# Index products of the sample tokens in 64x32 tiles, eight together, with buffers of their own for key/value turns and spread scores, and a third count on ScalarE

## The chip, the cores and the metric

One NeuronCore of a Trainium2 chip runs the whole kernel. The metric is the device time of one execution in microseconds. The kernel before took 988.06 us (median of three runs, 987.04 to 989.44).

The engines are named as in the profile: PE is TensorE, DVE is VectorE, ACT is ScalarE, POOL is GpSimd, SP is SyncE, which issues most DMAs. L913 is line 913 of the kernel.

## What is computed

The reference is one inference step of a hybrid decoder layer for 1024 prompt tokens and for 8 sequences of 4 sample tokens each (with 8192 past tokens in pages of 128). After an RMSNorm and one big input projection, a sparse attention and a retention run side by side; an output projection and a gate follow. The change touches how the sample tokens choose the 256 past tokens that they attend to:

```
def _index_select(qi, wi, ki, qpos, kpos, topk):
    s = jnp.einsum('bqhd,bsd->bqhs', qi, ki) * (D_IDX ** -0.5)     # 8 index heads, 64 wide
    score = jnp.einsum('bqh,bqhs->bqs', wi, jax.nn.relu(s))
    score = jnp.where(valid, score, -jnp.inf)
    top_val, top_idx = lax.top_k(score, topk)
```

For a sample sequence b, q runs over its 4 tokens and s over its 8192 past tokens, whose index keys lie in pages of a cache; so 32 rows (4 tokens x 8 heads) of 64 numbers meet 8192 keys. Besides, the prompt's own top 256 are found by a search that counts scores over a threshold, and the keys and values of the prompt are written out in token order.

## The kernel before

The kernel goes through stages in this order (times of the profiled execution): the norm, the transposes and the index projections and scores of the prompt (0 to 155 us); the **sample-index stage** (155 to 292 us); the retention (to about 555 us); the attention (to about 740 us); the output projection and the gate (to the end). The program is written as Python that emits instructions; a scheduler of the framework, which works on its own model of the time, then orders the instructions of each engine. Engines go through their instructions in that order and wait on one another by semaphores. issue_after (L880, L923) ties an instruction's place behind another's.

In the sample-index stage the loop at L904 goes through 16 page pairs (8 sequences, two halves a). For each:

- key_pages (L433) fetches 128 x 2048 numbers, 1 MB, by an indirect DMA that POOL issues (L437), into a slab kx. There are two slabs, so a load waits until the slab's last user is done.
- DVE turns the two halves of the slab by 32x32 blocks (L911, up = 0 and 1). The first result goes to the slab's free third, the second to a tile kT of its own.
- PE multiplies the queries with them (L913, into a pair of PSUM banks called pox; there are two such pairs). The stationary operand qbd is 128 x 64 per sequence: it holds the 32 query columns twice, for row half 0 in columns 0 to 31 and for row half 1 in columns 32 to 63, with zeros elsewhere. Each product takes all 128 rows and 64 columns of the array and streams 512 columns; the two for one half of the slab (u2 = 0 and 1) use the two column halves of the array. So a pair has 4 products (8 matmul records in the trace, since an fp32 matmul leaves two).
- ACT empties the banks with a Relu into rl (L916).

After two pairs, head_sum (L876) weighs and adds the heads: four products into the four 32-row strips of a bank py (L879, L882), a copy ys (L884), and a DMA to xt_d. Later by_key (L888) turns ys once more (xv, L890), spreads it on POOL (xe, L892) and writes it to xs_d. rn, ys, xv and xe share a ring of two buffers.

Between these, unit() runs the input projections of the queries (qa), keys and values (kava), and the gate (ga): a unit is 24 matmuls into a bank pb (L286 to L288) for 384, 416 or 256 tokens, and a consumer. Those of keys and values call use_kv (L462): a copy of pb into kvs on ACT (L465), and before the next unit turn_kv (L469): PE transposes (L474, into kvt), a copy back into the second half of kvs on DVE (L476), and one DMA of it to the output (L478; L497 writes values once more to v_d). kvs, qst (queries), kst (keys) and sga (gate) all take their buffers from one ring of two, tag qst.

The prompt's search (bisect_prompt) is stepped in between as well. A round counts, for six blocks of 128 prompt tokens, how many scores pass a threshold. The two longest blocks (1024 and 896 scores) are counted on ACT (L737, js), the other four on DVE (L739, jk); excess (L742) joins the counts on DVE, and a new threshold W follows. NA is the number of blocks counted on ACT.

Of the kernel before, what the change touches and what calls it, by code (L numbers as in the profile page):

```python
# [11 lines left out]
F32 = mybir.dt.float32  # L12
# [5 lines left out]
ALU = mybir.AluOpType  # L18
# [29 lines left out]
def _const_table():  # L48
# [15 lines left out]
    put("caus", caus)  # L64
    put("wsel", ((p // 8 % 4 * 4 + p // 32)[:, None] == np.arange(32)[None, :]) * 1.0)
    put("slots", np.tile(np.arange(256.0), (128, 1)))
# [65 lines left out]
def tile_step(ctx: ExitStack, tc: tile.TileContext, I, O):  # L132
# [271 lines left out]
    sx0 = sxs.enter_context(pool("sx0"))  # L404
    qbd = sx0.tile([128, 8, 64], F32, name="qbd")
    nc.gpsimd.memset(qbd, 0.0)
    kis = sx0.tile([64, NS], F32, name="kis")
    qsn = sx0.tile([64, 8, NS], F32, name="qsn")

    def q_sample_index(j, pt):  # L410
        for o in range(2):
            s = pt[o * 64:o * 64 + 64, 384:416].rearrange("p (b t) -> p b t", b=8)
            for r in range(2):
                d = qbd[r * 64:r * 64 + 64].rearrange("p b (r t h) -> p r b t h", r=2, h=8)
                nc.vector.tensor_scalar(d[:, r, :, :, 2 * j + o], s, 0.125, None, op0=ALU.mult)
            nc.vector.tensor_scalar(qsn[:, 2 * j + o, :], pt[o * 64:o * 64 + 64, 384:416], 0.125, None, op0=ALU.mult)
# [45 lines left out]
    def use_kv(g, pt, outs, outp, new, then=lambda tk: None):  # L462

        st = qsp.tile([128, 2, 416], F32, tag="qst", bufs=2, name="kvs")
        nc.scalar.copy(st[:, 0, :GRP[g][1]], pt[:, :GRP[g][1]])  # L465
        turn.append(lambda: then(turn_kv(g, st, outs, outp, new)))

    def turn_kv(g, st, outs, outp, new):
# [6 lines left out]
        nb = NP[g]  # L475
        nc.vector.tensor_copy(st[:, 1, :nb], tp[:, :nb])  # L476
        tk = st[:, 1, :nb].rearrange("p (b c) -> p b c", c=128)
# [218 lines left out]
    NB = 6  # L696
    NA = 2

# [157 lines left out]
    def step(gen, n=1):  # L856
        for _ in range(n):
# [4 lines left out]

    wst = sx.tile([128, 8, 32], F32, name="wst")
    nc.vector.tensor_tensor(wst, wcol[:, :, None].to_broadcast([128, 8, 32]),
                            C("wsel")[:, None, :].to_broadcast([128, 8, 32]), op=ALU.mult)
    pn = bank("pn", "t")
# [9 lines left out]
    def head_sum(b, rls):  # L876
        py = bank("py")

        last_ = nc.tensor.matmul(py[96:128, :], wst[:, b, :], rls[3], start=True, stop=True)  # L879
        with tc.issue_after(last_.ins):  # L880
            for i in range(3):
                nc.tensor.matmul(py[32 * i:32 * i + 32, :], wst[:, b, :], rls[i], start=True, stop=True)  # L882
        ys = sx.tile([128, 512], F32, tag="ys", bufs=2, name="ys")
        nc.scalar.copy(ys, py)  # L884
        nc.sync.dma_start(xt_d[b], ys)
        pend.append(lambda: by_key(b, ys))

    def by_key(b, ys):  # L888
        xv = sx.tile([128, 512], F32, tag="ys", bufs=2, name="xv")
        nc.vector.transpose(xv, ys)  # L890
        xe = sx.tile([128, 8, 16, 2], F32, tag="ys", bufs=2, name="xe")
        nc.gpsimd.tensor_copy(xe.rearrange("p c k r -> p k c r"),  # L892
# [11 lines left out]
    for b in range(8):  # L904
        rls = []
        for a in range(2):
            kx = key_pages(2 * b + a) if b else kxs[a]
            po = pair("pox")
            for up in range(2):
                kT = kx[:, 2048:] if up == 0 else sx.tile([128, 1024], F32, tag="kT", bufs=1, name="kT")  # L910
                nc.vector.transpose(kT, kx[:, up * 1024:up * 1024 + 1024])  # L911
                for u2 in range(2):
                    nc.tensor.matmul(po[u2 * 64:u2 * 64 + 64, up * 512:up * 512 + 512], qbd[:, b, :],  # L913
                                     kT[:, u2 * 512:u2 * 512 + 512], start=True, stop=True)
            rl = sx.tile([128, 1024], F32, tag="rl", bufs=3, name="rl")
# [1164 lines left out]
```

## Time and profile before

| | |
|---|---|
| median of the runs | 988.06 us (987.04 to 989.44) |
| the profiled execution | 981.7 us, span 979.9 us |
| mean granted clock of PE | 0.991 |
| busy, share of the span | PE 95%, DVE 65%, ACT 46%, POOL 33% |
| sample-index stage, 155 to 292 us | PE 129.6, DVE 106.7, ACT 56.0, POOL 38.3 of 137 us |

The profile is that of one execution. Its rows give, per line, engine and pair of tiles, how often an instruction ran and how long it took; a bracket behind a row says how long the engine stood idle before it and which instruction ended that wait. The chain view follows the work that ended last backwards through what released it. The granted clock is the share of full speed that PE was allowed. Matmuls overlap, so the distance between the starts of two of them says more than the length of one.

### The profile page before, as it was taken

What the parts mean: (1) busy time and instruction counts of PE and PEld (TensorE: products, weight loads), DVE (VectorE), ACT (ScalarE), POOL (GpSimd) and SP (SyncE); (2) the same over time, 40 slices, a digit from 0 to 9 for tenths busy, and PEclk for the clock granted to TensorE, in tenths of its full rate; (3) what the DMA queues carried; (4) which work ended last, traced back from release to release, by engine and by line L of the source; (5) the groups of instructions that cost most, each with busy time, mean ns of one, the idle gap of its engine ahead of it and who ended that gap; (6) DMA issues with size and microseconds to landing.
All of it is one profiled execution on the core that took longest, in us unless ns stands there. A gap on an engine that the chain in (4) does not pass through costs nothing.

```text
span 979.9 us, 18935 instructions
## 1 busy us (share of the span) xinstructions
PE 927.9 (95%) x6980; PEld 788.2 (80%) x6980; DVE 640.3 (65%) x1917; ACT 450.9 (46%) x1002; POOL 319.3 (33%) x443
## 2 busy tenths in 40 slices
PE   4999999799999999999999978999999999999998
PEld 3988888567668988898989865666668999999998
DVE  6847768788945669988885577887644224953332
ACT  5646564345323886425334365565555334432210
POOL 4205112313406414415335136354414422033300
PEclk9999999899999999999999979999999999999999
DMA  8314225757534110333147226343212222512211
GB/s 267 121 67 112 71 65 181 268 171 250 161 128 107 44 44 24 88 76 79 33 132 200 83 67 183 100 124 85 61 58 80 93 66 76 176 64 88 94 35 38
DMA packets 102127, 104.36 MB, mean 107 GB/s; under 512 B 22002, under 2 KB 92210, under 8 KB 99602
## 3 DMA queue, kind: packets, MB, share of 16 engines
q1 hardware_dynamic: 96274, 76.93, 26.4%
q0 software_dynamic: 5760, 26.22, 8.8%
q8 instruction: 55, 0.90, 0.4%
q14 instruction: 38, 0.31, 0.1%
HBM read 80.36 MB, written 22.76 MB: 105 GB/s over the span
## 4 chain that ended last, share of the span: by engine, by line
PE 73%; DVE 11%; DMA 8%; ACT 4%; issue 2%; SPq 1%; POOL 0%; DVEq 0%; ACTq 0%; POOLq 0%
PE pb L286 5%; PE pb L288 4%; PE pb L287 4%; PE ob L1845 3%; PE ptp L1837 3%; PE pg L296 3%; PE pg L298 3%; PE pg L297 3%; PE pvg L296 3%; PE pvg L297 3%; PE pvg L298 3%; PE pqk L296 3%; PE pqk L297 3%; PE pqk L298 2%; PE po L296 2%; PE po L297 2%
## 5 line engine op out<-in xcount | busy, mean ns | idle before, releaser
L1308 POOL DMA_INDIRECT kvs<-in_cache_kv,idx x64 | 65.7, 1027 | 93.0 <-ACT pT L1842 29.6
L296 PE MATMUL pvg<-whi_vgb,xh 128*128 128x256 f32 x256 | 75.1, 293 | 0.6 <-DVE rp L1144 0.6
L296 PE MATMUL pqk<-whi_qkb,xh 128*128 128x256 f32 x256 | 73.4, 287 | 1.7 <-DVE rp L1144 1.2
L297 PE MATMUL pvg<-wlo_vgb,xh 128*128 128x256 f32 x256 | 73.7, 288 | 0.8 <-POOL wlo_vgb L201 0.8
L297 PE MATMUL pqk<-wlo_qkb,xh 128*128 128x256 f32 x256 | 73.6, 287 | 0.0
L296 PE MATMUL po<-whi_o,yTh 128*128 128x256 f32 x256 | 73.2, 286 | 0.2 <-ACT yTh L1892 0.2
L298 PE MATMUL pvg<-whi_vgb,xl 128*128 128x256 f32 x256 | 73.3, 286 | 0.0
L297 PE MATMUL po<-wlo_o,yTh 128*128 128x256 f32 x256 | 72.8, 284 | 0.0
L296 PE MATMUL pg<-whi_g,yTh 128*128 128x256 f32 x256 | 72.7, 284 | 0.0
L298 PE MATMUL po<-whi_o,yTl 128*128 128x256 f32 x256 | 72.7, 285 | 0.0
L298 PE MATMUL pqk<-whi_qkb,xl 128*128 128x256 f32 x256 | 72.7, 284 | 0.0
L298 PE MATMUL pg<-whi_g,yTl 128*128 128x256 f32 x256 | 72.3, 283 | 0.0
L297 PE MATMUL pg<-wlo_g,yTh 128*128 128x256 f32 x256 | 72.2, 282 | 0.0
L1824 ACT ACTIVATE L<-L,mn 128x128 f32<-128x128 f32 (+7 forms) x64 | 49.7, 777 | 19.4 <-DVE mn L1820 18.9
L201 POOL TENSOR_TENSOR wlo_g<-wraw_g,whi_g 128x256 fp32r<-128x256 f32 x32 | 27.2, 881 | 87.9 <-ACT whi_g L200 87.7
L2035 DVE TENSOR_TENSOR sgm<-pu,sgm 128x256 f32<-128x256 f32 x32 | 13.6, 424 | 64.2 <-PE pu L298 60.8
L296 PEld LDWEIGHTS pqk<-whi_qkb,xh 128*128 128x128 f32 x256 | 48.2, 188 | 3.2 <-issue 1.8
L296 PEld LDWEIGHTS po<-whi_o,yTh 128*128 128x128 f32 x256 | 49.0, 191 | 2.0 <-issue 1.6
L296 PEld LDWEIGHTS pvg<-whi_vgb,xh 128*128 128x128 f32 x256 | 48.4, 189 | 2.7 <-PE pvg L305 0.8
L296 PEld LDWEIGHTS pg<-whi_g,yTh 128*128 128x128 f32 x256 | 48.7, 190 | 1.6 <-issue 1.6
L1837 PEld LDWEIGHTS ptp<-cst,L 128*128 128x128 f32 x288 | 31.6, 142 | 22.6 <-issue 18.7
L297 PEld LDWEIGHTS pvg<-wlo_vgb,xh 128*128 128x128 f32 x256 | 48.3, 189 | 1.6 <-POOL wlo_vgb L201 1.0
(540 smaller groups left out, 3058.3 us busy)
## 6 DMA issues: line engine op xcount, KB each, us to landing
wraw_qkb<-in_w_in SPq DMA_DIRECT2D x16, 256.0 KB
wraw_vgb<-in_w_in SPq DMA_DIRECT2D x16, 256.0 KB
qas<-qas_d SPq DMA_DIRECT2D x8, 512.0 KB
wraw_o<-in_w_out SPq DMA_DIRECT2D x8, 512.0 KB
xr<-in_x_prompt SPq DMA_DIRECT2D x8, 512.0 KB
wraw_g<-in_w_ple_gate SPq DMA_DIRECT2D x8, 512.0 KB
out_y_prompt<-sgm SPq DMA_DIRECT2D x32, 128.0 KB
qas_d<-qst SPq DMA_DIRECT2D x8, 384.0 KB
```

Source lines behind the costliest of these rows:

```text
L201: nc.gpsimd.tensor_tensor(lo[:, k, :n], raw, hi[:, k, :n].bitcast(F32), op=ALU.subtract)
L286: nc.tensor.matmul(pt[:m, :n], wh, xh[:, k, ts], start=(k == 0), stop=False)
L287: nc.tensor.matmul(pt[:m, :n], wh, xl[:, k, ts], start=False, stop=False)
L288: nc.tensor.matmul(pt[:m, :n], wl, xh[:, k, ts], start=False, stop=(k == KC - 1))
L296: nc.tensor.matmul(pt[:, :n], ah, hi[:, k, :n], start=(k == 0), stop=False)
L297: nc.tensor.matmul(pt[:, :n], ah, lo[:, k, :n], start=False, stop=False)
L298: nc.tensor.matmul(pt[:, :n], al, hi[:, k, :n], start=False, stop=(k == kc - 1))
L1308: return nc.gpsimd.indirect_dma_start(out=dst, out_offset=None, in_=kvflat, in_offset=bass.IndirectOffsetOnAxis(ap=idx, axis=0))
L1824: behind[0] = nc.scalar.activation(L[:, :n], L[:, :n], AF.Exp, bias=least, scale=-1.0, accum_out=sm[:, i4:i4 + 1])
L1837: nc.tensor.transpose(tp[:, i4 * 128:i4 * 128 + 128], P[i4][:, kb * 128:kb * 128 + 128], ident)
L1845: nc.tensor.matmul(ob[64 * o:64 * o + 64, :256], vtok[:, kb, kv * 64:kv * 64 + 64], pT[:, o * 256:o * 256 + 256], start=(kb == 0), stop=(k ...
L2035: nc.vector.tensor_tensor(sg[:rows], usrc, sg[:rows], op=ALU.mult)
```

## The change

- The stationary operand becomes 64 rows by 32 columns: qbd is 128 x 8 x 32, each row half holds the 32 query columns, and there are no zeros to clear. Each page pair now has eight products (L920 in the changed kernel), one for each half of the slab (up), each 512 columns (u2) and each row half (r). Each has its own place among the array's two row halves and four column strips; up = 1 comes first, and each later product is put behind the first one.
- Both turns of a slab (L911) now come ahead of the products, and both results stay in the slab, so kT is gone and a slab is in use until all eight products are through.
- The row halves of up = 1 write swapped strips, so the rows of rl are ordered otherwise for it. wsel and wst, which pick the heads' weights, get a second version (wsel1), and head_sum uses wst[:, 1] for up = 1.
- kvs leaves the qst ring for one buffer of its own, and the copy back from kvt moves from DVE to ACT (L477 now).
- xe leaves the ys ring for one buffer of its own.
- NA goes from 2 to 3: the block with 768 scores is counted on ACT.

```
-    put("wsel", ((p // 8 % 4 * 4 + p // 32)[:, None] == np.arange(32)[None, :]) * 1.0)
+    for up in range(2):
+        slot = p // 8 % 4 * 4 + p // 32 % 2 * 2 + (p // 64 ^ up)
+        put(f"wsel{up}", (slot[:, None] == np.arange(32)[None, :]) * 1.0)
...
-    qbd = sx0.tile([128, 8, 64], F32, name="qbd")
-    nc.gpsimd.memset(qbd, 0.0)
+    qbd = sx0.tile([128, 8, 32], F32, name="qbd")
...
-        st = qsp.tile([128, 2, 416], F32, tag="qst", bufs=2, name="kvs")
+        st = sx.tile([128, 2, 416], F32, tag="kvs", bufs=1, name="kvs")
...
-        nc.vector.tensor_copy(st[:, 1, :nb], tp[:, :nb])
+        nc.scalar.copy(st[:, 1, :nb], tp[:, :nb])
...
-    NA = 2
+    NA = 3
...
-        last_ = nc.tensor.matmul(py[96:128, :], wst[:, b, :], rls[3], start=True, stop=True)
+        last_ = nc.tensor.matmul(py[96:128, :], wst[:, 1, b, :], rls[3], start=True, stop=True)
...
-                nc.tensor.matmul(py[32 * i:32 * i + 32, :], wst[:, b, :], rls[i], start=True, stop=True)
+                nc.tensor.matmul(py[32 * i:32 * i + 32, :], wst[:, i % 2, b, :], rls[i], start=True, stop=True)
...
-        xe = sx.tile([128, 8, 16, 2], F32, tag="ys", bufs=2, name="xe")
+        xe = sx.tile([128, 8, 16, 2], F32, tag="xe", bufs=1, name="xe")
...
+            kT = (kx[:, 2048:], kx[:, :1024])
             for up in range(2):
-                kT = kx[:, 2048:] if up == 0 else sx.tile([128, 1024], F32, tag="kT", bufs=1, name="kT")
-                nc.vector.transpose(kT, kx[:, up * 1024:up * 1024 + 1024])
+                nc.vector.transpose(kT[up], kx[:, up * 1024:up * 1024 + 1024])
+            head = None
+            for up in (1, 0):
                 for u2 in range(2):
-                    nc.tensor.matmul(po[u2 * 64:u2 * 64 + 64, up * 512:up * 512 + 512], qbd[:, b, :],
-                                     kT[:, u2 * 512:u2 * 512 + 512], start=True, stop=True)
+                    for r in range(2):
+                        o, rr = 32 * (2 * (r ^ up) + u2), slice(r * 64, r * 64 + 64)
+                        with (tc.issue_after(head) if head else ExitStack()):
+                            mm = nc.tensor.matmul(po[o:o + 32, up * 512:up * 512 + 512], qbd[rr, b, :],
+                                                  kT[up][rr, u2 * 512:u2 * 512 + 512], start=True, stop=True,
+                                                  tile_position=(64 * r, o))
+                        head = head or mm.ins
```

The order of the instructions moves with it. PE's order is the same up to the stage's second group of products and again in the retention; inside the stage, and in parts of the attention, it differs. Of the 16 page pairs, 13 now have their eight products in one piece; three are split by other work on PE (seven and one, five and three, three and five).

First PE, at the fourth page pair (the first unit of the keys and values ends just before, the second follows). Before, each half of a slab has its products (x2) by itself, and those of the fifth pair's first half come behind py:

```order
L288 MATMUL pb<-xh,wlo_kava 128x384
L913 MATMUL pox<-kx,qbd 64x512 x2
L913 MATMUL pox<-kT,qbd 64x512 x2
L879 MATMUL py<-rl,wst 32x512
L882 MATMUL py<-rl,wst 32x512 x3
L913 MATMUL pox<-kx,qbd 64x512 x2
L474 MATMUL kvt<-cst,kvs 128x128 x3
L286 MATMUL pb<-xh,whi_kava 128x416
```

After the change, at the same place (the eighth product of the third pair and all eight of the fourth):

```order
L290 MATMUL pb<-xh,wlo_kava 128x384
L920 MATMUL pox<-kx,qbd 32x512 x9
L881 MATMUL py<-rl,wst 32x512
L884 MATMUL py<-rl,wst 32x512 x3
L475 MATMUL kvt<-cst,kvs 128x128 x3
L288 MATMUL pb<-xh,whi_kava 128x416
```

The products of a pair have come together, and no product of the fifth pair stands ahead of kvt any more.

Then ACT at the same place, with the engines and queues that each instruction waits for. Before, the first copy into kvs:

```order
L487 CAST kst_1801<-pb_1776 128x384 [waits DMAHW4_49,PE_49]
L465 COPY kvs_1805<-pb_1776 128x384 [waits DMAHW6_49,DVE_49]
L916 ACTIVATE rl_1938<-pox_1930 128x1024 [waits PE_49]
L884 COPY ys_1824<-py_1819 128x512 [waits PE_49]
L737 ACTIVATE js_1717,cnt_1597<-score_97,W_1594 128x1024 [waits DVE_49]
L737 ACTIVATE js_1719,cnt_1597<-score_97,W_1594 128x896 [waits Activation_49]
```

After:

```order
L466 COPY kvs_1811<-pb_1782 128x384 [waits DVE_49]
L738 ACTIVATE js_1723,cnt_1600<-score_97,W_1597 128x1024 [waits DVE_49,Activation_49]
L925 ACTIVATE rl_1950<-pox_1939 128x1024 [waits PE_49]
L738 ACTIVATE js_1725,cnt_1600<-score_97,W_1597 128x896 [waits Activation_49]
L886 COPY ys_1833<-py_1828 128x512 [waits PE_49]
L477 COPY kvs_1811<-kvt_1859 128x384 [waits PE_49]
L738 ACTIVATE js_1727,cnt_1600<-score_97,W_1597 128x768 [waits Activation_49]
```

The first copy has lost its wait for a DMA queue (DMAHW), a third count has come in, and so has the copy back from kvt.

Last, ACT a little further on, in the units of keys and values that follow. Before:

```order
L487 CAST kst_1922<-pb_1897 128x256 [waits DMAHW4_49]
L465 COPY kvs_1926<-pb_1897 128x256 [waits DMAHW5_49,DVE_49,PE_49]
L465 COPY kvs_2021<-pb_1996 128x384 [waits DMAHW7_49,PE_49,Activation_49]
L737 ACTIVATE js_1956,cnt_1597<-score_97,W_1594 128x1024 [waits DVE_49]
L737 ACTIVATE js_1958,cnt_1597<-score_97,W_1594 128x896 [waits Activation_49]
L465 COPY kvs_2055<-pb_2030 128x416 [waits DMAHW0_49,PE_49]
```

After:

```order
L466 COPY kvs_1935<-pb_1906 128x256 [waits DMAHW6_49]
L477 COPY kvs_1935<-kvt_2003 128x256 [waits PE_49]
L738 ACTIVATE js_1968,cnt_1600<-score_97,W_1597 128x1024 [waits DVE_49,Activation_49]
L738 ACTIVATE js_1970,cnt_1600<-score_97,W_1597 128x896 [waits Activation_49]
L738 ACTIVATE js_1972,cnt_1600<-score_97,W_1597 128x768 [waits Activation_49]
L466 COPY kvs_2033<-pb_2008 128x384 [waits DMAHW0_49]
L477 COPY kvs_2033<-kvt_2035 128x384 [waits PE_49]
```

Each copy into kvs now waits for the DMA that writes out the unit before it, since there is one buffer, and the copy out of kvt stands between.

More of the change, by code (lines that the diff above doesn't have):

```diff
@@ L413, in q_sample_index @@
             for r in range(2):
-                d = qbd[r * 64:r * 64 + 64].rearrange("p b (r t h) -> p r b t h", r=2, h=8)
-                nc.vector.tensor_scalar(d[:, r, :, :, 2 * j + o], s, 0.125, None, op0=ALU.mult)
+                d = qbd[r * 64:r * 64 + 64].rearrange("p b (t h) -> p b t h", h=8)
+                nc.vector.tensor_scalar(d[:, :, :, 2 * j + o], s, 0.125, None, op0=ALU.mult)
             nc.vector.tensor_scalar(qsn[:, 2 * j + o, :], pt[o * 64:o * 64 + 64, 384:416], 0.125, None, op0=ALU.mult)
@@ L861, in tile_step @@
     sx = sxs.enter_context(pool("sx", side="right"))
-    wst = sx.tile([128, 8, 32], F32, name="wst")
-    nc.vector.tensor_tensor(wst, wcol[:, :, None].to_broadcast([128, 8, 32]),
-                            C("wsel")[:, None, :].to_broadcast([128, 8, 32]), op=ALU.mult)
+    wst = sx.tile([128, 2, 8, 32], F32, name="wst")
+    for up in range(2):
+        nc.vector.tensor_tensor(wst[:, up], wcol[:, :, None].to_broadcast([128, 8, 32]),
+                                C(f"wsel{up}")[:, None, :].to_broadcast([128, 8, 32]), op=ALU.mult)
     pn = bank("pn", "t")
```

## The prediction

> **What bounds the kernel now.** I read the page first: the engines' shares and the chain that ended last.
>
> ```profile
> span 979.9 us, 18935 instructions
> PE 927.9 (95%) x6980; PEld 788.2 (80%) x6980; DVE 640.3 (65%) x1917; ACT 450.9 (46%) x1002; POOL 319.3 (33%) x443
> PE 73%; DVE 11%; DMA 8%; ACT 4%; issue 2%; SPq 1%; POOL 0%; DVEq 0%; ACTq 0%; POOLq 0%
> ```
>
> TensorE (PE) is busy for 95% of the span and carries 73% of the chain, so time that the change takes off PE counts almost in full. All the edits lie in the sample-index stage, whose products run from 155 to 292 us. The windows view gives that stage, its worst stretch, and the stretch behind it:
>
> ```profile
> core 0: us, PE busy (x) PEld busy (x) DVE busy (x) ACT busy (x) POOL busy (x), PEclk, DMA share, GB/s
> 155.00:292.00 137.00, 129.58 (x735) 92.86 (x737) 106.67 (x243) 55.98 (x89) 38.27 (x52) 0.98 0.62 201
> 183.00:192.00 9.00, 3.68 (x13) 3.56 (x14) 4.13 (x10) 4.16 (x7) 0.94 (x1) 0.62 0.99 362
> 300.00:320.00 20.00, 18.18 (x154) 16.72 (x152) 14.22 (x39) 8.81 (x13) 13.39 (x20) 1.00 0.35 80
> ```
>
> PE idles 7.4 of the stage's 137 us (137.00 - 129.58); DVE is busy for 107, ScalarE (ACT) for 56. Most of the idling lies in 183 to 192, where PE does 3.68 us of work at a granted clock of 0.62. So there are two things to win here: PE's own work, and one stall.
>
> **The index products.** The lines for the tiles pox and rl, and PE's timeline round a lone group of products (start, us, instruction; one product leaves two records):
>
> ```profile
> L913 PE MATMUL pox<-kx,qbd x64: 592/592/644, 155.7 to 281.3; 128*64 128x512 f32 x64
> L913 PE MATMUL pox<-kT,qbd x64: 592/592/644, 161.1 to 285.8; 128*64 128x512 f32 x64
> L916 ACT ACTIVATE rl<-pox x16: 1007/1027/1044, 162.3 to 286.4; 128x1024 f32<-128x1024 f32 x16
> ...
> 218.05 0.28 PE L287 MATMUL pb<-xl,whi_kava 128*128 128x256 f32 x1
> 218.18 0.28 PE L288 MATMUL pb<-xh,wlo_kava 128*128 128x256 f32 x1
> 218.38 1.08 PE L913 MATMUL pox<-kx,qbd 128*64 128x512 f32 x4
> 219.39 0.44 PE L286 MATMUL pb<-xh,whi_ga 128*128 128x384 f32 x1
> 219.67 0.33 PE L287 MATMUL pb<-xl,whi_ga 128*128 128x384 f32 x1
> 219.84 0.34 PE L288 MATMUL pb<-xh,wlo_ga 128*128 128x384 f32 x1
> ```
>
> Two products side by side hold PE for 1.01 us (218.38 to 219.39). Getting in and out costs some more: the step from 218.18 to 218.38 is 0.20 where these matmuls follow each other at 0.13, and from 219.39 to 219.67 it is 0.28 where the next step is 0.17, together 0.2 us a visit. Where two groups follow directly the chain has 1.87, so each further group adds 0.86:
>
> ```profile
> 218.46 1.01 PE pox L913 x4
> 234.80 1.87 PE pox L913 x8
> ```
>
> The 128 records stand in 24 visits: 18 of one group, 4 of two, 2 of three. That is 18 x 1.01 + 4 x 1.87 + 2 x 2.73 = 31.1 us, plus 24 x 0.2 = 4.8: **35.9 us**.
>
> After the change a page pair is eight products, each of 64 rows and 32 columns of the array, each at a place of its own, with all 512 columns of keys still streaming through each. No row of this trace shows eight. Two rows of its kind bound it: four column strips run together in head_sum, and two row halves run together in the retention:
>
> ```profile
> 225.17 0.62 PE L879 MATMUL py<-rl,wst 128*32 128x512 f32 x1
> 225.18 0.63 PE L882 MATMUL py<-rl,wst 128*32 128x512 f32 x3
> 225.62 0.59 PE L879 MATMUL py<-rl,wst 128*32 128x512 f32 x1
> 225.63 0.61 PE L882 MATMUL py<-rl,wst 128*32 128x512 f32 x3
> 226.17 1.08 PE L913 MATMUL pox<-kx,qbd 128*64 128x512 f32 x4
> ...
> 333.02 0.37 PE L1173 MATMUL ret<-qkT 64*128 64x128 f32 x1
> 333.02 0.37 PE L1173 MATMUL second<-qkT 64*128 64x128 f32 x1
> ```
>
> Four strips with 512 columns take 225.17 to 226.17, 1.00 us, as long as two. The halves start in the same 10 ns. If strips and halves combine, eight products take about 1.06 us (1.01 and six more starts of some 8 ns). The ends are 1.06 us and eight in a row, 1.01 + 7 x 0.86 = 7.0 us. I take 1.06: both halves of the claim have a row.
>
> The new order keeps 13 of the 16 pairs whole; three are split (7 + 1, 5 + 3, 3 + 5), and two of the pieces stand next to another pair. That makes 17 visits, 15 of about 1.06 and 2 of about 1.92 (a second round): 19.7 us, plus 17 x 0.2 = 3.4: **23.1 us, so 12.8 less**. PE runs into nothing else here: rl (1.03 us a pair, 16 us of 137) still empties each pair of banks.
>
> [...]
>
> **The stall at 183.** PE's timeline, ACT's, and the chain there:
>
> ```profile
> 188.32 0.90 PE L474 MATMUL kvt<-cst,kvs 128*128 128x128 f32 x3 [5.42 <-ACT kvs L465]
> 187.79 0.48 ACT L465 COPY kvs<-pb 128x384 f32<-128x384 f32 x1 [9.18 <-DMA qas_d<-qst]
> 180.13 7.58 DMA qas_d<-qst
> ...
> 189.22 0.35 PE pb L286
> 192.12 0.19 PE pb L286
> ```
>
> The copy into kvs (L465) takes a buffer of the qst ring, whose last owner is still being written to qas_d (7.58 us, DMA engines 0.99 busy). ACT waits 9.18 us, PE behind it 5.42. Then PE's clock is half: eight matmuls at about 0.35 apart in place of 0.19, 1.3 us. With a buffer of its own the first kvs waits for no DMA. **Gain 5.4 + 1.3 = 6.7 us**, if nothing else is late there.
>
> **What is late next.** The price of the slab and of the single kvs buffer, from the waits and the lines (the first landing row is that of the key pages, the second that of all DMAs of tiles named kvs, later gathers of that name among them):
>
> ```profile
> POOL kx L437 <- PE pox L913: 17.1, 4, 8.0
> POOL xe L892 <- DMA xt_d<-ys: 21.4, 3, 8.5
> DMA to landing us min/median/max: 5.7/6.1/8.5
> L911 DVE STREAM_TRANSPOSE kx<-kx x16: 1228/1245/1248, 106.9 to 277.2; 128x1024 f32<-128x1024 f32 x16
> ...
> L465 ACT COPY kvs<-pb x6: 362/481/493, 187.8 to 220.3; 128x384 f32<-128x384 f32 x2, 128x416 f32<-128x416 f32 x2, 128x256 f32<-128x256 f32 x2
> L476 DVE COPY kvs<-kvt x6: 387/520/558, 189.3 to 226.7; 128x384 f32<-128x384 f32 x4, 128x256 f32<-128x256 f32 x2
> DMA to landing us min/median/max: 2.6/2.8/6.7
> ```
>
> *Key pages.* A slab is now free only after all eight products. From there to the next products of that slab: landing 6.1 (5.7 to 8.5) and two transposes, 2.5; 8.6 us at best. What PE has to do meanwhile is, by the new order and 0.12, 0.175 and 0.19 us a matmul (24 matmuls: 2.8, 4.2 or 4.5), 10 to 18 us at 11 places. It is some 8 at the second pair (pox_1699 to pox_1939), 7.5 at pox_2154 to pox_2306. At pox_2071 it is 10, but its load is issued behind the straggling eighth product of pox_1815 and the rounding of a weight tile on POOL. I put 1 us on each, 3 us; the ends are 0 and 7 (the 8.5 us landing at all three). In return xe has its own buffer, so the kx loads behind xe on POOL no longer stand through its 21.4 us of waits.
>
> *The single kvs buffer.* From the second unit on, L465 waits until the unit before has been transposed (0.5), copied (0.5, now on ACT) and written (2.6 to 6.7, for values twice over): 4 to 8 us, against 5 to 7 us of PE work between. ACT stands in order, so the counts, the Relu copies and the projections' copies queue behind that wait. Five such places, 0 to 3 us each; most lie nearer to the cover, so I take 0.6 each, 3 us.
>
> *The counts and copies.*
>
> ```profile
> L737 ACT ACTIVATE js<-score,W x14: 1034/1096/1172, 169.1 to 240.7; 128x1024 bf16<-128x1024 f32 x7, 128x896 bf16<-128x896 f32 x7
> L739 DVE TENSOR_SCALAR_CACHE_REDUCE jk<-score,W x28: 557/792/1015, 169.1 to 245.7; 128x768 bf16<-128x768 f32 x7, 128x640 bf16<-128x640 f32 x7, 128x512 bf16<-128x512 f32 x7, 128x384 bf16<-128x384 f32 x7
> ```
>
> DVE loses seven counts of 1.0 us and six copies of 0.5, some 10 us, and gains one small product for wst. ACT gains about the same: 67 of perhaps 123 us. Neither bounds the stage, so the sum takes 0. If ACT is late with the third count, DVE's step of the search (L746) stands, and with it the transposes behind it: I count that inside the 3 us for key pages. The memset of qbd lay long before; nothing.
>
> **The sum.** -12.8 - 6.7 + 3 + 3 = **-13.5 us**. Behind the stage PE is nearly full and the order of the retention is unchanged, so the gain moves through; in the attention the order is reshuffled, which I take as 0, with ends of 3 either way. On the profiled execution, 981.7 us, this makes 968.2; that one lies 6.4 under the median of 988.06, and the forecast is made on the median: **974.5 us**.
>
> **The rivals.**
>
> *Waits give much of it back* (chance 0.20). The upper ends: 7 us for pages and 10 for kvs instead of 3 + 3, which leaves 2.5 to 8 of gain: 980 to 985.5. For it: DMA at 0.99 busy round 183 to 192, so a page that PE asks for earlier may just land late. Against: DMA is 0.62 busy over the stage.
>
> *No new waits, and more* (0.14). The 6 us of waits don't come, and the half-clock stretch in the attention goes as well (570 to 581 here, granted clock 0.53, where DVE and ACT are the late ones):
>
> ```profile
> 570.00:581.00 11.00, 9.67 (x46) 8.15 (x46) 8.76 (x45) 5.05 (x19) 0.00 (x0) 0.53 0.24 71
> ```
>
> -12.8 - 6.7 = -19.5, and up to 4 more: 964 to 969.
>
> *The row halves of a bank take turns* (0.05), the slower one. If PE starts a product only when the one before it in the same bank, from the other row half, is through, the program's order (the halves alternate, one bank after the other) puts all eight in a row: 7.0 us a pair, 16 x 7.0 + 3.4 = 115 in place of 35.9. That is +79, less the 6.7: about 1060. It decides from 2.1 us a pair on ((35.9 + 6.7 - 6 - 3.4) / 16), that is as soon as a pair takes more than two rounds.
>
> *The eight run in two rounds* (0.03), or the stall only changes its name: pairs at 1.92 as now, 16 x 1.92 + 3.4 = 34; gain 2 + 6.7 - 6, or 985.
>
> **How the numbers follow.** Forecast 974.5 (969 to 980): 0.55; waits: 0.20; more: 0.14; turns: 0.05; two rounds: 0.03; and 0.03 for a reshuffled attention that costs over 10 us. A difference under 0.2% (2 us) cannot be told from none. From 986 to 990 lies 0.04, from the ends of the wait and two-round cases; slower has the turns and 0.02 of the attention, 0.07; faster 0.89. The range leaves out the turns, the rest of the slower cases and the outer ends: **965 to 985**.
>
> **What would show it.** Right: eight pox records within 0.1 us of each other, pox busy 17 to 20 us in the stage; no idle before the first kvt; products of the last pair at about 272 us in place of 285; new idle of PE before pox_1939, pox_2071, pox_2306 released by DVE kx, and before kvt by ACT kvs, 6 us in all. Wrong: pox records one after another (turns); PE idle in the stage still 7 us or more with other releasers; a later stage that grows.

## The result and the profile after

The changed kernel took **980.73 us** (median of 22 runs, 977.5 to 990.53) where the kernel before took 987.97 (22 runs, 982.91 to 992.59). The ratio is 0.9942, with an interval of 0.9929 to 0.9956, or 5.7 us less. The ratio is that of the means (982.0 and 987.7 us); the two medians lie 7.2 us apart. The time lies in the forecast's range, and the sign is right, but by the ratio the gain is less than half of the 13.5 us. The profiled execution took 980.64 us, with a span of 978.8 and a mean granted clock of 0.981 (0.991 before). It lies only 1.1 us under the profiled execution of before, since that one, 981.7 us, is below all 22 runs compared here (982.91 at the lowest).

The page's shares, and then the windows view of the stretches shown of before, with one more (220 to 230):

```profile
PE 925.4 (95%) x7108; PEld 790.9 (81%) x7108; DVE 636.4 (65%) x1898; ACT 458.3 (47%) x1022; POOL 315.6 (32%) x442
```

```profile
core 0: us, PE busy (x) PEld busy (x) DVE busy (x) ACT busy (x) POOL busy (x), PEclk, DMA share, GB/s
155.00:292.00 137.00, 124.67 (x915) 96.18 (x914) 103.07 (x229) 65.44 (x110) 42.10 (x63) 0.98 0.65 210
183.00:192.00 9.00, 8.56 (x45) 8.36 (x46) 6.89 (x21) 5.74 (x11) 1.35 (x2) 0.81 0.95 329
220.00:230.00 10.00, 6.55 (x41) 4.08 (x40) 7.44 (x21) 7.91 (x13) 4.55 (x7) 0.83 0.82 239
300.00:320.00 20.00, 20.00 (x171) 18.78 (x170) 16.59 (x45) 14.13 (x24) 10.57 (x22) 1.00 0.27 66
```

PE does 8.56 us of work in 183 to 192 where it did 3.68, and the stretch in the retention (300 to 320) is full where it was busy for 18.18. But at 220 to 230 there is a new hole. Whole windows hide that the stage itself became shorter, so here are the stages by their first products. "Stage" is from the first index product to the first projection product of the retention (pqk), and idle is PE's idle time in it; "front" runs from there to the first pvg product; "attention" from the last pvg to the first product of the output projection.

| us, profiled executions | stage | idle | front | attention |
|---|---|---|---|---|
| before | 135.9 | 7.4 | 27.4 | 185.6 |
| changed | 129.6 | 12.3 | 24.9 | 193.2 |
| difference | -6.3 | +4.9 | -2.5 | +7.6 |

The other stretches differ by 0.9 us at most. In the stage, PE's busy time fell by 11.2 us (128.5 to 117.3), and 4.9 of that became idle time.

The attention's 7.6 us are not more idle time of PE. These are its windows, before and then changed:

```profile
557.35:742.99 185.64, 173.86 (x1320) 114.50 (x1318) 128.44 (x486) 104.98 (x238) 77.79 (x81) 0.97 0.33 94
549.51:742.75 193.24, 183.48 (x1319) 119.91 (x1318) 128.28 (x486) 104.40 (x238) 77.77 (x81) 0.92 0.32 91
```

PE does the same work there (1320 and 1319 records) and idles less (9.8 us where it was 11.8), but is busy for 9.6 us more at a lower granted clock, 0.92 for 0.97.

**The products.** PE's timeline round one pair and at the last one, then the tile pox alone in the stage (its busy time, records, clock), of the changed kernel:

```profile
270.07 1.09 PE L920 MATMUL pox<-kx,qbd 64*32 64x512 f32 x16
271.10 0.62 PE L881 MATMUL py<-rl,wst 128*32 128x512 f32 x1
277.63 1.09 PE L920 MATMUL pox<-kx,qbd 64*32 64x512 f32 x16
```

```profile
155.00:287.00 132.00, 20.28 (x256) 0.97 0.65 210
```

All 16 records of a pair's eight products fall in 1.09 us, and what follows starts 1.03 us after the first (270.07 to 271.10). The same row of the kernel before has 32.98 us:

```profile
155.00:287.00 132.00, 32.98 (x128) 0.97 0.64 207
```

**The waits.** The rows of PE's timeline in the stage with an idle time before them (two are left out, of 0.15 and 0.35 us):

```profile
162.57 0.43 PE L288 MATMUL pb<-xh,whi_qa 128*128 128x416 f32 x1 [0.68 <-DVE qst L379]
169.34 0.36 PE L288 MATMUL pb<-xh,whi_qa 128*128 128x256 f32 x1 [0.96 <-DVE qst L379]
183.44 0.55 PE L475 MATMUL kvt<-cst,kvs 128*128 128x128 f32 x3 [2.39 <-ACT kvs L466]
195.08 0.66 PE L475 MATMUL kvt<-cst,kvs 128*128 128x128 f32 x4 [1.14 <-ACT kvs L466]
201.32 0.44 PE L475 MATMUL kvt<-cst,kvs 128*128 128x128 f32 x2 [0.35 <-ACT kvs L466]
208.36 0.55 PE L475 MATMUL kvt<-cst,kvs 128*128 128x128 f32 x3 [1.05 <-ACT kvs L466]
211.03 1.09 PE L920 MATMUL pox<-kx,qbd 64*32 64x512 f32 x16 [1.13 <-ACT rl L925]
215.76 0.66 PE L475 MATMUL kvt<-cst,kvs 128*128 128x128 f32 x4 [0.62 <-ACT kvs L466]
225.09 0.62 PE L881 MATMUL py<-rl,wst 128*32 128x512 f32 x1 [3.44 <-ACT sga L503]
```

ACT releases seven of the nine. Its own rows at the two longest, and DVE's row behind which the copy into kvs stood:

```profile
182.90 0.48 ACT L466 COPY kvs<-pb 128x384 f32<-128x384 f32 x1 [2.85 <-DVE kst L489]
194.52 0.51 ACT L466 COPY kvs<-pb 128x416 f32<-128x416 f32 x1 [1.19 <-DMA out_k_prompt<-kvs]
...
221.99 1.15 ACT L738 ACTIVATE js<-score,W 128x1024 bf16<-128x1024 f32 x1 [3.10 <-DVE W L771]
223.25 1.28 ACT L503 ACT_TABLE_LOAD   x1
224.55 0.49 ACT L503 ACTIVATE sga<-pb 128x384 f32<-128x384 f32 x1
```

```profile
179.50 0.78 DVE L763 TENSOR_SCALAR far<-W 128x6 int32<-128x6 f32 x1
180.31 0.67 DVE L764 COPY_PREDICATED W<-far,W 128x24 f32<-128x24 int32 x1
181.02 0.63 DVE L766 TENSOR_TENSOR wd<-W 128x12 f32<-128x12 f32 x1
...
182.31 0.56 DVE L489 TENSOR_TENSOR kst<-pb,kst 128x384 fp32r<-128x384 f32 x1
```

At 183 the copy into kvs no longer waits for a DMA. It waits for DVE's subtraction L489, which reads the same bank pb, and that stands behind a run of small steps of the prompt's search (L763 to L769). At 222 ACT stands 3.10 us in a count (L738) that needs the search's new threshold; the gate's activation queued behind it, a table load of 1.28 us included, is what PE waits for.

On a second chip the changed kernel measured 974.19 against 982.16, a ratio of 0.9921 (0.9902 to 0.9941), with one more profile of each kernel:

| us | stage | idle | front | attention |
|---|---|---|---|---|
| before, again | 136.0 | 7.3 | 27.5 | 184.5 |
| changed, again | 129.9 | 12.9 | 25.2 | 187.2 |

Here the stage and the front repeat to 0.3 us. The attention doesn't. A third profile of the kernel before, on another chip (e5 below), has a stage of 138.1, so differences of about 2 us between single stages on different chips prove little.

### The profile page after: what moved, and what is told of

Read it like the earlier page. It is cut to its first block, busy times and chain, and to the rows that moved or that the text cites. A ratio compares the mean times of both kernels' runs of the same rounds, so it can differ in the third digit from the quotient of the medians.

```text
span 978.8 us, 19191 instructions
## 1 busy us (share of the span) xinstructions
PE 925.4 (95%) x7108; PEld 790.9 (81%) x7108; DVE 636.4 (65%) x1898; ACT 458.3 (47%) x1022; POOL 315.6 (32%) x442
## 4 chain that ended last, share of the span: by engine, by line
PE 61%; DVE 4%; DMA 3%; issue 2%; ACT 1%; POOL 1%; SPq 0%; ACTq 0%; DVEq 0%; POOLq 0%
PE ptp L1846 3%; PE ob L1854 3%; PE pg L298 3%; PE pg L300 3%; PE pg L299 3%; PE pvg L298 3%; PE po L298 3%; PE pvg L299 3%; PE po L299 3%; PE po L300 3%; PE pqk L298 3%; PE pvg L300 3%; PE pqk L299 3%; PE pqk L300 3%; PE sa L1823 2%; PE sa L1824 2%
## 5 line engine op out<-in xcount | busy, mean ns | idle before, releaser
L2043 ACT ACTIVATE sgm<-pg 128x256 f32<-128x256 f32 x32 | 12.3, 384 | 79.2 <-PE pg L300 74.2
```

Source lines behind the costliest of these rows:

```text
L2043: nc.scalar.activation(sg[:rows], gsrc, AF.Sigmoid)
```

## The experiments

The questions were why PE's saved time turned into waits, and what happened in the attention. The letters in the expectations stand for these theories. A: PE waits for ACT and DVE, in the order in which their instructions now stand. B: the supply is the limit, as key pages (B1) or as DVE's work (B2). M: several suppliers lie close behind PE, so that taking away one shows the next. S: the order of the program as a whole decides. For the attention: P, it differs by chip and execution; K, the change itself costs there; D, its end is tied to something with a time of its own. All ratios are to the kernel before, on the same chip.

**Parts of the change.** The first kernel is the kernel before with the index tiles alone (and so both turns in the slab); the second is the changed kernel with the four old products (128 x 64); the third is the changed kernel with two counts on ACT; the fourth gives the copy into kvs and the copy out of kvt a buffer each:

```diff
# e2_old_products
-    qbd = sx0.tile([128, 8, 32], F32, name="qbd")
+    qbd = sx0.tile([128, 8, 64], F32, name="qbd")
...
+                    nc.tensor.matmul(po[u2 * 64:u2 * 64 + 64, up * 512:up * 512 + 512], qbd[:, b, :],
+                                     kT[up][:, u2 * 512:u2 * 512 + 512], start=True, stop=True)
# e3_two_counts
-    NA = 3
+    NA = 2
# e4_kvs_split
-        st = sx.tile([128, 2, 416], F32, tag="kvs", bufs=1, name="kvs")
+        st = sx.tile([128, 416], F32, tag="kvi", bufs=1, name="kvi")
...
+        ko = sx.tile([128, 384], F32, tag="kvs", bufs=1, name="kvs")
+        nc.scalar.copy(ko[:, :nb], tp[:, :nb])
```

> Only the eight products together (with both turns in the slab); kvs in the qst ring, the copy back on DVE, xe in the ys ring and two counts on ACT as before. The stage from the first index product to the first product of the retention took 135.9 us before and 129.6 after. Theory A (PE's saving is real, the other edits' waits on ACT and DVE eat it): PE's 12.8 us come off, the 5.4 us stall stays, stage 123 to 126, so better than the whole change; time 4 to 8 us under the changed kernel's. Theory B (with less PE work the supply of key pages, DMA and DVE turns, sets the stage): stage 129 to 132 with other waits, time equal to the changed kernel's or above.

> All of the change but the tiles: four products of 128x64 a pair, both turns first, with kvs's own buffer, both copies and three counts on ACT, xe's own buffer. Theory A: the products' 12.8 us come back on top of the same waits, stage 138 to 143, time at or over that of the kernel before. Theory B: PE's longer work covers the waits, stage 130 to 135, time within 3 us of the changed kernel's.

> The whole change but for the third count on ACT (two as before). In the changed kernel PE waited 3.4 us before py at 221.7 us for a gate copy on ACT that stood behind a count, which waited 3.1 us for DVE's threshold; then the clock was at 0.66 for 5 us (1.7 us lost). Theory A: that wait goes, stage 123 to 126, time 3 to 6 us under the changed kernel's. Theory B: the wait moves to DVE's turns, stage 128 to 131, time within 2 us of the changed kernel's.

> The whole change, with kvs as two tiles of one buffer each (the copy from pb, and the copy from kvt that is written out), so that the next copy from pb waits for PE's transposes and no longer for a DMA. In the changed kernel PE stood 1.14, 0.35, 1.05 and 0.62 us for kvs copies that waited for these DMAs. Theory A: 2.5 to 3.5 us go, stage 126 to 127, time 2 to 4 us under the changed kernel's. Theory B: PE reaches the next wait earlier, stage 129 to 130, time equal.

| | ratio | stage | idle |
|---|---|---|---|
| e1_tiles_only | 0.9933 (0.9909 to 0.9957) | 132.1 | 14.8 |
| e2_old_products | 0.9941 (0.9921 to 0.9960) | 130.1 | 4.7 |
| e3_two_counts | 0.9973 (0.9947 to 0.9999) | 129.3 | 14.0 |
| e4_kvs_split | 0.9942 (0.9918 to 0.9967) | 127.1 | 12.6 |

The tiles alone win 3.8 us of the stage, the other edits alone 5.8, and both together 6.3. The gains don't add, and the ratios say the same of the whole time: 0.9933, 0.9941 and 0.9942. With the tiles alone PE's work falls by 11.2 us (128.5 to 117.3) and 7.4 of that become idle. The old and the new products under the same other edits, in one window (e2_old_products, then the changed kernel):

```profile
157.00:287.00 130.00, 125.25 (x717) 91.20 (x720) 97.89 (x221) 64.38 (x108) 37.85 (x51) 1.00 0.64 212
```

```profile
157.00:287.00 130.00, 117.67 (x861) 89.75 (x845) 99.70 (x221) 64.62 (x108) 37.03 (x51) 0.97 0.65 213
```

PE does 7.6 us less and idles as much longer, and its clock falls from 1.00 to 0.97. DVE's and ACT's work is the same within 2 us. So under the other edits something beside PE sets the stage's length. It is not the third count alone: in e3 the 3.44 us before py are gone, but two waits before kvt grow, from 2.39 and 0.62 us to 3.11 and 1.67, and the stage is the same. Nor is it the single kvs buffer alone: e4 wins 2.5 us of the stage (its time is that of the changed kernel), and then shows the waits for key pages that the changed kernel hid, of 0.58, 2.77 and 1.05 us (PE's timeline at the first kvt, where 1.95 us stay, and at two of the three; then ACT's copy for that kvt, which still waits for DVE's subtraction):

```profile
183.55 0.55 PE L475 MATMUL kvt<-cst,kvi 128*128 128x128 f32 x3 [1.95 <-issue]
255.13 1.09 PE L921 MATMUL pox<-kx,qbd 64*32 64x512 f32 x16 [2.77 <-DVE kx L914]
267.19 1.09 PE L921 MATMUL pox<-kx,qbd 64*32 64x512 f32 x16 [1.05 <-DVE kx L914]
183.02 0.48 ACT L466 COPY kvi<-pb 128x384 f32<-128x384 f32 x1 [2.42 <-DVE kst L490]
```

Of the forecasts, B's stages came in e1 (0.1 us over), e2 and e3, and A's missed in all three; e4's stage is nearer to A's, but its time didn't fall as A had it.

**One supplier taken away.** Beside one more profile of the kernel before (e5_before_again), the changed kernel without the later page loads, with DVE's counts over 64 scores only, and with the second turn left out. Each leaves out that part of the computation:

```diff
# e6_no_loads
-            kx = key_pages(2 * b + a) if b else kxs[a]
+            kx = kxs[a]
# e7_short_counts
-                    V.tensor_scalar(junk()[:, :n], sc, tj, None, op0=ALU.is_ge, op1=ALU.add,
+                    V.tensor_scalar(junk()[:, :64], sc[:, :64], tj, None, op0=ALU.is_ge, op1=ALU.add,
# e8_one_turn
-            kT = (kx[:, 2048:], kx[:, :1024])
-            for up in range(2):
-                nc.vector.transpose(kT[up], kx[:, up * 1024:up * 1024 + 1024])
+            kT = (kx[:, 2048:], kx[:, 1024:2048])
+            nc.vector.transpose(kT[0], kx[:, :1024])
```

> The kernel before once more, for a second profile. From its last retention projection to its first output product the first profile took 185.6 us, and the changed kernel and four variants of it 191 to 193. If the first profile was a fortunate execution (981.7 us where the runs have a median of 987), this one shows 189 to 193 there and the same stage, 135 to 137 us. If the changed order of the attention costs these 6 us, it shows 185 to 187.

> The changed kernel without the key-page loads from the third on: the products use the first two slabs again and again (the sample scores are therefore not the reference's, and the exact repair of ties is switched off); turns and products all stay. Theory B1 (the loop of slab free, load, two turns, products sets the stage): the stage falls from 129.6 to 116 to 121 us. Theory B2 (DVE, busy for 85 to 90% of 156 to 260, sets it by its order): 126 to 129. Theory A (ACT's order): 126 to 129, with the same waits before kvt and py.

> The changed kernel with DVE's counts of the prompt's search over 64 scores instead of 384 to 640 (the prompt's threshold is therefore not the reference's, and the exact repair is switched off): DVE loses some 11 us of work between 165 and 245 us. Theory B2: the stage falls by 6 to 10 us, to 120 to 124. Theory B1: by 0 to 3. Theory A: the waits of ACT for DVE's threshold shorten, 2 to 4 us.

> The changed kernel with one of the two turns of each slab left out (the second half goes to the products unturned, so half of the sample scores are not the reference's, and the exact repair is switched off): DVE loses 16 x 1.245 = 20 us, and the loop of a slab 1.25 us. Theory B2: the stage falls by 8 to 13 us. Theory B1: by 3 to 6. Theory A: by 0 to 3.

| | us | ratio | stage | idle | attention |
|---|---|---|---|---|---|
| e5_before_again | 988.58 | one execution | 138.1 | 8.5 | 188.7 |
| e6_no_loads | 980.12 | 0.9938 (0.9913 to 0.9964) | 129.8 | 10.6 | 192.8 |
| e7_short_counts | 982.6 | 0.9961 (0.9936 to 0.9987) | 131.7 | 11.5 | 191.8 |
| e8_one_turn | 985.81 | 0.9996 (0.9975 to 1.0018) | 133.8 | 12.0 | 192.8 |

No single one brings the stage under the changed kernel's 129.6 us, though each takes away what a plain theory of supply names as the limit: B1 and B2 drop out as single causes (B1 had a fall of 8.6 us or more in e6, B2 of 6 or more in e7 and 8 or more in e8). A's forecasts missed as well (129.8 for at most 129 in e6, and no shorter stage in e7 and e8). Leaving out the second turn even made it longer. The changed kernel was not profiled on this chip, where the kernel before had 138.1, so a gain of some 2 us could be hidden here. The attention of e5, 188.7, lies between what a fortunate first profile (189 to 193) and a cost of the change (185 to 187) would give. Since the scheduler orders each of these programs anew, a few us of a stage can also be the order.

**All of them, and a mended order.** e11_split_first is e4 with the copy for the transposes (now kvi) issued ahead of the subtraction that reads the same bank:

```diff
         t0, nb = GRP[g][0], NP[g]
+        use_kv(g, pt, O["k_sample"], O["k_prompt"], knew)
         st = qsp.tile([128, 2, 384], F32R, tag="qst", bufs=2, name="kst")
...
-        use_kv(g, pt, O["k_sample"], O["k_prompt"], knew)
```

e12_split_first_na2 is that with two counts on ACT. e9_relief is e11 without the later loads and the turns and with all counts over 64 scores; e10_relief_old is the same with the four old products. These two leave out that work and ask how long PE itself needs.

> The changed kernel with all that PE waited for taken away together: no key-page loads after the second, no turns of the slabs, all counts of the prompt's search over 64 scores, kvs split in two tiles and copied ahead of the keys' own copy (so neither the sample scores nor the prompt's thresholds are the reference's, and the exact repairs are switched off). Single removals left the stage at 127 to 134 us with 10 to 14 us of PE idle in it. Theory M (several suppliers, each only a few us behind PE, so that one that goes is followed by the next): the stage falls to 114 to 119 us, PE idle under 4. Theory S (PE's static order itself makes it wait): the stage stays over 124.

> The same with the four 128x64 products a pair as before in place of the eight tiles. Theory M: PE alone sets the stage now, so the tiles show their full worth, 11 to 13 us of stage more than with them, 126 to 131 us. Theory S: within 4 us of the run with tiles.

> The changed kernel with kvs as two tiles and its copy from pb ahead of the keys' own copy, so that it waits neither for a DMA nor for DVE. The whole result is computed. Theory M: 2 us of the wait before the first kvt go (1.95 in the split run) and part comes back elsewhere, stage 125 to 127.5, time 1 to 4 us under the changed kernel's. Theory S: 127 to 130, time equal.

> The same with two counts on ACT as before. The whole result is computed. Theory M: ACT has 7 us less, DVE 7 us more; with DVE busy for 85 to 90% the turns come later, stage 125 to 130. If ACT's order was the larger part: 123 to 125 and time 4 us under the changed kernel's.

| | us | ratio | stage | idle | attention |
|---|---|---|---|---|---|
| e9_relief | 966.34 | 0.9840 (0.9803 to 0.9878) | 123.0 | 3.3 | 184.6 |
| e10_relief_old | 970.43 | 0.9893 (0.9860 to 0.9925) | 126.8 | 0.0 | 184.1 |
| e11_split_first | 968.15 | 0.9860 (0.9834 to 0.9886) | 125.5 | 8.2 | 185.8 |
| e12_split_first_na2 | 976.47 | 0.9941 (0.9920 to 0.9962) | 130.2 | 14.0 | 184.8 |

The window of e10_relief_old, then that of e9_relief:

```profile
157.00:283.00 126.00, 126.00 (x712) 92.39 (x716) 53.62 (x189) 50.64 (x108) 22.57 (x36) 1.00 0.30 101
```

```profile
157.00:283.00 126.00, 122.65 (x876) 92.69 (x869) 55.15 (x192) 50.92 (x107) 23.72 (x41) 0.99 0.32 106
```

With the suppliers out of the way together, PE with the old products is busy without a gap: 126.8 us is the length that its own work sets, in this order. The stage of before, 135.9, lay only 9.1 above that. So without the tiles the other edits could win some 9 us, and they won 5.8. The tiles take 9.3 us off pox between these two kernels, in 16 and 21 visits (the tile's rows, e10 and then e9):

```profile
155.00:300.00 145.00, 34.37 (x128) 1.00 0.36 110
```

```profile
155.00:300.00 145.00, 25.02 (x256) 0.99 0.36 110
```

Of these 9.3 us, 3.3 come back as idle time and some at the lower clock (0.99 of 123 us); 3.8 reach the stage.

Neither M nor S has both runs. M's part on the suppliers holds: with all of them short the idle time falls from 12.3 to 3.3 us, which no single one did, and e10's stage is in M's range. But e9's 123.0 is above M's 114 to 119 (S had over 124), and the tiles' worth of 3.8 us is S's "within 4", not M's 11 to 13. A part of that is the order: e9 needs 25.0 us for its products where the changed kernel needs 20.3. What else the order costs, no run separates.

The mended order of e11 shows it at the place of the forecast stall. ACT's timeline there, then PE's:

```profile
179.72 0.48 ACT L466 COPY kvi<-pb 128x384 f32<-128x384 f32 x1
180.09 0.49 ACT L490 CAST kst<-pb 128x384 fp32r<-128x384 f32 x1
180.46 1.04 ACT L926 ACTIVATE rl<-pox 128x1024 f32<-128x1024 f32 x1
184.04 1.15 ACT L739 ACTIVATE js<-score,W 128x1024 bf16<-128x1024 f32 x1 [2.54 <-DVE W L772]
```

```profile
170.58 0.36 PE L288 MATMUL pb<-xh,whi_qa 128*128 128x256 f32 x1 [2.26 <-DVE qst L379]
182.22 0.55 PE L475 MATMUL kvt<-cst,kvi 128*128 128x128 f32 x3
183.93 0.46 PE L288 MATMUL pb<-xh,whi_kava 128*128 128x416 f32 x1 [1.17 <-DVE kst L491]
238.72 1.09 PE L921 MATMUL pox<-kx,qbd 64*32 64x512 f32 x16 [0.49 <-DVE kx L914]
252.07 1.96 PE L921 MATMUL pox<-kx,qbd 64*32 64x512 f32 x16 [2.98 <-DVE kx L914]
```

The copy is done 2.0 us before PE's kvt (179.72 + 0.48 to 182.22), and kvt has no idle time before it. The granted clock of 183 to 192 is 1.00 here. ACT still stands for the threshold (2.54), but PE has no wait for ACT here. What is left are 2.26 us for qst (0.96 in the changed kernel), 1.17 for the bank, and the key pages. The place in the program isn't all: in e9, with the same lines, the scheduler put a count, which needs the threshold, ahead of the copy, and kvt waited 1.72 us for the copy. With two counts on ACT (e12) the stage is 4.7 us longer, and the interval of its ratio lies above e11's: in this order the third count on ACT is worth having. M's stages came in e11, and in e12 within 0.2 us.

**The attention and the best version, on one chip.** e11 was run again beside the changed kernel and the kernel before, and with them the changed kernel with a delay: nine more products of 512 columns in the last head_sum, which write the same values again.

```diff
+        if b == 7:
+            for _ in range(9):
+                nc.tensor.matmul(py[96:128, :], wst[:, 1, b, :], rls[3], start=True, stop=True)
```

> The changed kernel once more, beside the next three on one chip. The stretch between the last retention projection and the first output product took 193.2 us in its first profile and 191 to 193 in the runs of the first two calls, but 184 to 186 in all four of the third call. Theory P (place and time: that stretch depends on the chip and the execution, not on the kernel): 184 to 193 here, and within 3 us of the kernel before's. Theory K (the changed kernel's own loss): 191 to 193 here, with the kernel before at 185 to 189. Stage 128 to 131 by both.

> The kernel before, a third profile, on the same chip as the other three. Theory P: its stretch between retention and output within 3 us of the changed kernel's. Theory K: 4 to 8 us under it. Stage 135 to 138 by both.

> The changed kernel with nine products added ahead of the last head_sum (they write what is written over behind them), some 8 us of PE work that bring PE to the retention as late as in the kernel before. Theory D (the attention waits for something that the stage does not bring forward, so an earlier arrival is lost there): the attention stretch falls by what was added, the total is that of the changed kernel within 3 us. Theory P or K: the stretch stays, the total grows by 7 to 9 us.

> The kernel with kvs in two tiles and its copy first, on the same chip as the changed kernel. On two chips the ratios to the kernel before were 0.986 for it and 0.994 for the changed kernel. Theory M (its stage is 4 us shorter, nothing else): 3 to 5 us under the changed kernel. If the attention's loss is the changed kernel's own (K): 8 to 10 us under it.

| | us | ratio | stage | attention |
|---|---|---|---|---|
| f1_changed_again | 974.19 | 0.9921 (0.9902 to 0.9941) | 129.9 | 187.2 |
| f2_before_third | 981.02 | one execution | 136.0 | 184.5 |
| f3_delay | 983.18 | 1.0018 (0.9998 to 1.0039) | 137.9 | 184.5 |
| f4_split_first_again | 970.62 | 0.9893 (0.9868 to 0.9918) | 124.6 | 183.5 |

The delay lengthened the stage by 8.0 us and the kernel by 9.0, as P and K had it (7 to 9 us), so no end that is fixed in time swallows what the stage wins: D drops out. On this chip the attention's difference between the changed kernel and the one before is 2.7 us, not 7.6, and the two versions that differ from the changed kernel only in the stage have 183.5 and 184.5. The variants had 190.9 to 192.8 on two chips, where one profile of the kernel before, on one of them, had 188.7; on the two others they had 183.5 to 187.2, and the kernel before 184.5. So P explains a good part of the 7.6; some 4 us (192.8 - 188.7) may be the change's on those chips, and whether they are stays open.

e11's version is the fastest that does all the work, with 968.15 and 970.62 on two chips. On the chip that ran both it is 3.6 us below the changed kernel by the medians, with a stage 5.3 us shorter, as M had it (3 to 5 us of time) and not K (8 to 10); the intervals of the two ratios overlap a little there (0.9902 and 0.9918).

## Why the prediction was right on the products and wrong on the waits

The forecast for the stage was -13.5 us: PE's busy time -14.1 (12.8 and 1.3 of half clock), and idle time from 7.4 to 8.0 (less 5.4, plus 6). Measured were -11.2 of busy time and 12.3 of idle, hence -6.3. Of the 7.2 us between, 4.3 are idle time (12.3 - 8.0) and 2.9 busy time (14.1 - 11.2); 1.3 of that is the half clock that didn't go. So the step that failed is the one from PE's saved time to the stage's: "time that the change takes off PE counts almost in full". Two terms of the sum show where, the stall at 183 and the counts and copies.

- *The products*: right in kind, and near in size. 17 visits, as forecast, and 20.28 us of pox, a little over the 17 to 20. This row fell by 12.7 us; that the sum had 12.8 is in part luck, since 1.4 of it stood for the steps in and out of fewer visits, and 11.4 (31.1 - 19.7) for the products themselves. Both halves of the claim held together: column strips and row halves at once, 1.03 us a pair. The rival of the row halves has nothing for it: eight products in a row would make 7.0 us a pair (1.01 + 7 x 0.86), and here, with strips from both row halves in each bank, what follows a pair's products starts 1.03 us after the first of them (270.07 to 271.10).
- *The stall at 183*: **the step failed**, in its condition "if nothing else is late there". It had 6.7 us. The wait for the DMA went, as said, but DVE's subtraction was late too, and 2.39 us of 5.42 stayed. So did a stretch of half clock behind it (0.50 in 185 to 188, 0.81 over 183 to 192). The order in front of the prediction had it: the copy's row still said "waits DVE_49". The price of that one row was never taken. ACT stood 2.85 us for that subtraction, which reads the same bank; why the two reads are put in order, no run shows. Moving the copy ahead of the subtraction, on top of the split buffer, took the wait away (e11), where the split buffer alone left 1.95 us (e4).
- *The counts and copies, priced at 0 because "Neither bounds the stage"*: **the step failed**, and this is the larger one. ACT is busy for 65 of 137 us, as forecast, and still ends the longest wait (3.44 us at 225, with 0.83 of the clock in 220 to 230), since it goes through its instructions in order and a count that waits for DVE (3.10 us, to 221.99) holds what is behind it (the gate's activation, at 224.55). Add 1.13 before rl, where "PE runs into nothing else here" was the reading. A share of busy time says nothing of that. The third count by itself isn't what the stage pays for: with two (e3) the 3.44 us are gone and the stage is as long. The two waits for qst, 1.6 us, had no term either; they end on DVE and come with the tiles alone as well (0.65 and 1.49 us in e1). And DVE lost 5.8 us of work in the stage (106.1 to 100.2) where some 10 were forecast.
- *The single kvs buffer*: right in size. Four waits of PE, 1.14 + 0.35 + 1.05 + 0.62 = 3.2 us where 3 was forecast, with ACT standing for the DMA of the unit before (1.19, twice).
- *Key pages*: 3 us forecast, none measured in the changed kernel, where the other waits gave the loads time. They came when some of those waits were gone: 4.4 us in e4, 3.5 in e11.
- *The gain moves through*: right, and there was more. The front lost two waits that stood in the kernel before:

```profile
307.88 0.35 PE L296 MATMUL pqk<-whi_qkb,xh 128*128 128x256 f32 x1 [0.50 <-DVE ssm L1028]
312.61 0.36 PE L296 MATMUL pqk<-whi_qkb,xh 128*128 128x256 f32 x1 [1.22 <-DVE rp L1144]
```

  They are 1.7 of the 2.5 us that the front won, which no term had.
- *The attention at 0, with 3 either way*: 2.7 on one chip, inside; 7.6 in the first pair of profiles, outside.

Of the signs, the last pair's products came at 277.6 and not at 272, and the idle time before the first kvt did not go. Two signs of being wrong came: PE idle in the stage for over 7 us with other releasers, and a later stage that grew, the attention. The rival "waits give much of it back" has the size that came (980 to 985.5), though with other waits than it named.

Behind both terms stands the one reading: "time that the change takes off PE counts almost in full" was taken from a busy share of 95% over the whole span. In this stage it held for the tiles at two fifths of their size at best: 3.8 of 11.2 us without the other edits (e1), 0.5 under them (e2), 3.8 of 9.3 with every supplier cut short (e9 and e10).

## What to carry to other kernels

Before a large saving on the bounding engine is counted, ask how far behind it the next supplier is. Run the stage with the suppliers cut short, and with the old work on the bounding engine; here that gave 9.1 us for the suppliers and 3.8 for the tiles, where the sum had 13.5 and 5.7 came. Where an edit takes away the last of several waits, price each of the others printed beside it. On an engine that works in order, as ACT did here (3.10 us of a count's wait ahead of the gate's activation), price not its load but what stands behind each instruction that waits, and put the copies that others need ahead of the counts that wait.

## What was unexpected of the hardware

In the changed kernel's attention a half-clock stretch lasted far longer than the wait ahead of it. PE waited 1.75 us, then had a granted clock of 0.51 for 20.48 us, though it is listed as busy for all of it (timeline, then windows):

```profile
553.01 0.53 PE L1681 MATMUL ret<-vv,qk 128*128 128x128 f32 x2 [1.75 <-DVE sm L1183]
```

```profile
549.60:553.01 3.41, 1.66 (x14) 1.09 (x12) 3.32 (x6) 2.52 (x4) 1.97 (x2) 1.00 0.51 129
553.01:573.49 20.48, 20.48 (x110) 16.99 (x112) 14.02 (x72) 9.48 (x34) 5.52 (x8) 0.51 0.28 75
573.49:576.90 3.41, 3.41 (x30) 2.26 (x26) 3.41 (x13) 2.88 (x7) 2.73 (x3) 0.95 0.14 41
```

PE left 110 matmul records in those 20.48 us, and the 3.41 us behind them had a clock of 0.95. What in that stretch kept the clock down was not tried.
